# Moving mask adds, query and rotary products to VectorE and key copies to ScalarE in a hybrid two-layer trunk

## The chip, the cores and the metric

The kernel runs on one NeuronCore of a Trainium2 chip. The metric is the device time of one launch in microseconds (us). A core has TensorE (PE in the profile) for matrix products, VectorE (DVE), ScalarE (ACT) and GpSimd (POOL) for elementwise work, and SyncE (SP), which issues the DMA transfers here. Each engine executes its own instructions in the order of the program and waits on semaphores for the others.

## The reference

Two layers run over 640 tokens: 512 of a denoising group and 128 of a context group. Cut to what matters:

```python
h = rmsnorm(x, norm1) * (1 + sc1) + sh1
proj = h @ w_in + b_in          # columns: da_q, da_k, da_v, ml_q..ml_g, na_q, na_k, na_v, merge
# DA: differential attention, 4 heads; rope_2d on q and k of the denoising group; softmax(q1 k1) - lam softmax(q2 k2)
# ML: bidirectional mLSTM, 4 heads, 2 directions; per chunk
sc  = einsum(q, k) * exp(logd - m_t)          # logd is -inf outside the causal triangle
num = inter * einsum(q, c) + einsum(sc, v)    # inter: the decay of the carried state
# NA: neighbourhood attention, 8 heads in 4 pairs, window bias and context keys
x = x + g1 * (merged projections of the three mixers)
x = x + g2 * (relu(h2 @ w_ff1) ** 2 @ w_ff2)
```

All of it is float32; the kernel multiplies in three passes of high and low halves.

## The kernel before, in words

A token tile is 128 tokens; a layer has five, four of the denoising group and one of the context (TT = 5, NT = 640, NS = 512). The weights arrive by DMA in blocks of 1 MB. ScalarE casts a block to its high half (whi, L217), VectorE subtracts to get the low half (wlo, L218), and TensorE multiplies high by high, high by low and low by high (L191 to L193, L210 to L212). The results lie in PSUM banks named mm, of which there are two (NMM = 2); each is evacuated by an instruction of a mixer, such as L620 on VectorE (an mLSTM key plus bias), L454 on ScalarE (a merge gate: bias and tanh), or L501 and L503 on VectorE (merged sums). A new projection group can start when its bank has been evacuated.

A layer runs its mixers as stages: ML, DA, NA, and then the MLP. In each, a driver interleaves the steps of the mixer with projection units for the stage after it, in the order in which the code is traced; a scheduler then orders each engine's instructions by it. In the background of the ML stage VectorE forms the modulation vectors of the next block in chunks of 512 columns (L323, on macc). The four parts of the code that matter:

- **ml_prep** (L732 to L751) fetches what the next head needs: for each of two directions the 128x640 row M (L739, a broadcast DMA from rd), to which a causal mask mlm is added (L741); the 128x512 decay of the queries (L744); and the carried state C. It runs once before the first head, and then within a head (after its second chunk) for the next.
- **ml_stages** (from L753): ScalarE takes exponentials of the masked rows (L768), the scores s = k q are formed, the decays are multiplied with the queries (L776), the scores with the exponentials (L778). Then, chunk by chunk, TensorE updates the state (L808), VectorE adds the decayed old state (L816), TensorE forms the outputs (L826, L828), and VectorE normalises them (L835 to L837, L842, L844). The rotating buffers of the head come from hd().
- **stack** (L919 to L950) prepares keys and queries of a DA head or NA pair. For each half j, the key's high part goes into one half of the partitions of k (L937, and L939 for the 128 cached keys in DA), is copied into the other half (L940); the low part is formed on VectorE (L942, L944) and copied likewise (L945). The copies are 64x640 in DA and 64x512 in NA. Zeroed context keys Kc are formed on GpSimd (L933 to L936).
- **da_rope** (L952 to L959) rotates a head's query or key: a shuffle by 16 partitions (L956), a product with the sines (L957), one with the cosines (L958), and a sum (L959).

In the NA stage GpSimd also forms the window tables (comb, L1216 and L1220), normalises the weights (L1294) and adds gated branches (L504).

Of the kernel before, what the change touches and what calls it, by code (L numbers as in the profile page):

```python
# [11 lines left out]
F32 = mybir.dt.float32  # L12
F32R = mybir.dt.float32r
AF = mybir.ActivationFunctionType
ALU = mybir.AluOpType
# [4 lines left out]
P = 128  # L20
# [3 lines left out]
NS = 512  # L24
NT = 640
TT = 5
# [60 lines left out]
class Builder:  # L87
# [644 lines left out]
    def ml_prep(self, l, h):  # L732
        nc, I = self.nc, self.I
        cv = self.colv[l][0]
        (cA, cB), rd, decb = self.mlc
        Mb, ib, C = [], [], []
        for dr in range(2):
            m = self.hd()
            nc.sync.dma_start(m, rd[0, dr, h].partition_broadcast(P))  # L739
            m3 = m.rearrange("p (c t) -> p c t", c=TT)  # L740
            nc.gpsimd.tensor_tensor(m3, m3, self.mlm[dr].unsqueeze(1).to_broadcast([P, TT, P]), op=ALU.add)  # L741
            Mb.append(m)
            i_ = self.hd()
            nc.sync.dma_start(i_[:, :NS], rd[1, dr, h, 0:NS].partition_broadcast(P))  # L744
            ib.append(i_)
            cst = self.T(self.sp, [P, 129], F32, "C", 8)
            nc.sync.dma_start(cst[:, :P], I["state_ml_C"][0, l, dr, h])
            nc.gpsimd.tensor_copy(cst[:, P:P + 1], cv[:, ROW_SN + 4 * dr + h:ROW_SN + 4 * dr + h + 1])
            C.append(cst)
        return Mb, ib, C  # L750

    def ml_stages(self, l):
        nc, I, O = self.nc, self.I, self.O  # L753
# [8 lines left out]
        for h in range(4):  # L762
            Mb, qs, C = nxt
# [6 lines left out]
            kT, qT = self.mlt.pop(("k", h)), self.mlt.pop(("q", h))  # L770
# [2 lines left out]
                sl = slice(c * P, (c + 1) * P)  # L773
                nc.tensor.matmul(sp[:, sl], kT[:, sl], qT[:, sl], start=True, stop=True)
            for dr in range(2):
                nc.gpsimd.tensor_tensor(qs[dr][:, :NS], qs[dr][:, :NS], qT[:, :NS], op=ALU.mult)  # L776
            for dr in range(2):
                nc.vector.tensor_tensor(Mb[dr], sp[:, :NT], Mb[dr], op=ALU.mult)  # L778
            yield
# [139 lines left out]
    def stack(self, qT, kT, more=None, cache=None):  # L919

        nc = self.nc
        Q, K, Kl = [], [], []
        Kc = self.hd()[:, :512].rearrange("p (j n) -> p j n", j=2)
        nk = NS if more is None else NT
        halves = (slice(0, 64), slice(64, 128))
        for j in range(2):
            a, b = halves[j], halves[1 - j]
            q = self.T(self.sp, [P, NS], F32R, "stq", 2)  # L930
            k = self.T(self.sp, [P, nk], F32R, "stk", 2)
            kl = self.hd(F32R)[:, :nk]
            nc.gpsimd.memset(Kc[b, j], 0.0)  # L933
            nc.gpsimd.tensor_copy(Kc[a, j, :P], kT[a, NS:])
            if cache is not None:
                nc.gpsimd.tensor_copy(Kc[a, j, P:], cache[a])  # L936
            nc.scalar.copy(k[a, :NS], kT[a, :NS])  # L937
            if more is not None:
                nc.scalar.copy(k[a, NS:], more[a])  # L939
            nc.gpsimd.tensor_copy(k[b], k[a].bitcast(F32))  # L940
            nc.scalar.copy(q[a], qT[a, :NS])
            nc.vector.tensor_tensor(kl[a, :NS], kT[a, :NS], k[a, :NS].bitcast(F32), op=ALU.subtract)  # L942
            if more is not None:
                nc.vector.tensor_tensor(kl[a, NS:], more[a], k[a, NS:].bitcast(F32), op=ALU.subtract)  # L944
            nc.gpsimd.tensor_copy(kl[b], kl[a].bitcast(F32))  # L945
            nc.vector.tensor_tensor(q[b], qT[a, :NS], q[a].bitcast(F32), op=ALU.subtract)
            Q.append(q)
            K.append(k)
            Kl.append(kl)
        return dict(qT=qT, Q=Q, K=K, Kl=Kl, Kc=Kc)  # L950

    def da_rope(self, x):  # L952
        nc = self.nc
        cos, sin = self.rope
        sw = self.hd()
        nc.vector.stream_shuffle(sw[:, :NS], x[:, :NS], [i ^ 16 for i in range(32)])  # L956
        nc.gpsimd.tensor_tensor(sw[:, :NS], sw[:, :NS], sin, op=ALU.mult)  # L957
        nc.vector.tensor_tensor(x[:, :NS], x[:, :NS], cos, op=ALU.mult)  # L958
        nc.vector.tensor_tensor(x[:, :NS], x[:, :NS], sw[:, :NS], op=ALU.add)  # L959

# [835 lines left out]
```

## Time and profile before

| | |
|---|---|
| median of 3 runs | 2478.33 us (2477.34 to 2484.72) |
| profiled execution | 2481.89 us, of which the span from the first to the last instruction is 2480.1 us |
| mean granted TensorE clock | 0.994 |
| TensorE busy | 2413.0 us (97%) |
| VectorE busy | 1523.1 us (61%) |
| ScalarE busy | 908.6 us (37%) |
| GpSimd busy | 646.9 us (26%) |

The busy times say how much work an engine had, not whether anyone waited for it. TensorE is busy nearly throughout, so the time is TensorE's work and the places at which it stands still. From the windows one reads how much it stands still in a stretch, from the list of its waits what each of them ended on, and from the timelines what the engine that it waited for was doing. The ML stage of layer 0 lies between 62 and 266 us, its DA stage up to 462 and its NA stage up to 690 us; those of layer 1 follow between 1305 and 1920 us.

### The profile page before, as it was taken

What the parts mean: (1) busy time and instruction counts of PE and PEld (TensorE: products, weight loads), DVE (VectorE), ACT (ScalarE), POOL (GpSimd) and SP (SyncE); (2) the same over time, 40 slices, a digit from 0 to 9 for tenths busy, and PEclk for the clock granted to TensorE, in tenths of its full rate; (3) what the DMA queues carried; (4) which work ended last, traced back from release to release, by engine and by line L of the source; (5) the groups of instructions that cost most, each with busy time, mean ns of one, the idle gap of its engine ahead of it and who ended that gap; (6) DMA issues with size and microseconds to landing.
All of it is one profiled execution on the core that took longest, in us unless ns stands there. A gap on an engine that the chain in (4) does not pass through costs nothing.

```text
span 2480.1 us, 39537 instructions
## 1 busy us (share of the span) xinstructions
PE 2413.0 (97%) x15776; PEld 2265.3 (91%) x15776; DVE 1523.1 (61%) x2788; ACT 908.6 (37%) x1954; POOL 646.9 (26%) x703
## 2 busy tenths in 40 slices
PE   6999999999999999999999999999999999999998
PEld 4999999999998898999989999999989889999997
DVE  5567788566634899998565547664443464444444
ACT  4333344343433422232353334443443353322232
POOL 0122122233412233332022222212351312233301
PEclk8999999999999999999999999999999999999999
DMA  7333323433353334444332322223232722121211
GB/s 268 109 102 110 114 103 131 128 110 129 133 195 126 119 136 151 156 136 153 103 122 98 108 85 80 80 79 114 71 117 85 262 85 85 69 85 69 85 68 60
DMA packets 73706, 286.52 MB, mean 116 GB/s; under 512 B 9889, under 2 KB 21249, under 8 KB 49969
## 3 DMA queue, kind: packets, MB, share of 16 engines
q1 hardware_dynamic: 73520, 283.99, 33.3%
q8 instruction: 124, 2.03, 0.3%
q14 instruction: 62, 0.50, 0.1%
HBM read 257.60 MB, written 26.35 MB: 114 GB/s over the span
## 4 chain that ended last, share of the span: by engine, by line
PE 61%; issue 2%; DVE 2%; POOL 2%; DMA 1%; ACT 1%; SPq 0%; POOLq 0%; DVEq 0%
PE mm L191 9%; PE mm L192 9%; PE mm L193 9%; PE mm L212 4%; PE mm L210 4%; PE mm L211 4%; PE t L210 3%; PE t L212 3%; PE t L211 3%; PE t L193 2%; PE t L192 2%; PE t L191 2%; PE t L1034 1%; PE t L1322 1%; PE s L210 1%
## 5 line engine op out<-in xcount | busy, mean ns | idle before, releaser
L191 PE MATMUL mm<-act,whi 128*128 128x384 f32 (+1 forms) x2160 | 693.0, 321 | 8.2 <-DVE act L503 3.4
L192 PE MATMUL mm<-act,whi 128*128 128x384 f32 (+1 forms) x2160 | 681.4, 315 | 0.0
L193 PE MATMUL mm<-act,wlo 128*128 128x384 f32 (+1 forms) x2160 | 681.1, 315 | 0.0
L217 ACT CAST whi<-raw 128x1024 fp32r<-128x1024 f32 x296 | 310.8, 1050 | 893.7 <-PE mm L192 417.7
L218 DVE TENSOR_TENSOR wlo<-raw,whi 128x1024 fp32r<-128x1024 f32 x296 | 384.0, 1297 | 358.7 <-ACT whi L217 304.9
L191 PEld LDWEIGHTS mm<-act,whi 128*128 128x128 f32 x2160 | 409.7, 190 | 13.2 <-issue 3.8
L192 PEld LDWEIGHTS mm<-act,whi 128*128 128x128 f32 x2160 | 410.0, 190 | 0.0
L193 PEld LDWEIGHTS mm<-act,wlo 128*128 128x128 f32 x2160 | 409.3, 190 | 0.0
L1544 POOL TENSOR_TENSOR x<-x,tmp 128x512 f32<-128x512 f32 x120 | 193.8, 1621 | 449.0 <-DVE tmp L1543 449.0
L210 PE MATMUL mm<-whi,act 128*128 128x512 f32 (+2 forms) x768 | 261.8, 341 | 0.0
L211 PE MATMUL mm<-wlo,act 128*128 128x512 f32 (+2 forms) x768 | 258.2, 336 | 0.0
L212 PE MATMUL mm<-whi,act 128*128 128x512 f32 (+2 forms) x768 | 258.1, 336 | 0.0
L323 DVE SCALAR_TENSOR_TENSOR macc<-raw,cc,macc 128x512 f32<-128x512 f32 x280 | 231.7, 871 | 21.0 <-DMA raw<-w_mod 20.7
L210 PE MATMUL t<-whi,act 128*128 128x512 f32 (+2 forms) x448 | 167.6, 374 | 1.6 <-ACT act L217 1.5
L211 PE MATMUL t<-wlo,act 128*128 128x512 f32 (+2 forms) x448 | 167.0, 373 | 0.0
L212 PE MATMUL t<-whi,act 128*128 128x512 f32 (+2 forms) x448 | 166.8, 372 | 0.0
L212 PEld LDWEIGHTS mm<-whi,act 128*128 128x128 f32 x768 | 146.4, 191 | 14.3
L210 PEld LDWEIGHTS mm<-whi,act 128*128 128x128 f32 x768 | 146.7, 191 | 14.0
L211 PEld LDWEIGHTS mm<-wlo,act 128*128 128x128 f32 x768 | 146.6, 191 | 14.1
L192 PE MATMUL t<-act,whi 128*128 128x256 f32 (+1 forms) x528 | 150.9, 286 | 0.0
L193 PE MATMUL t<-act,wlo 128*128 128x256 f32 (+1 forms) x528 | 150.9, 286 | 0.0
L191 PE MATMUL t<-act,whi 128*128 128x256 f32 (+1 forms) x528 | 150.7, 286 | 0.0
(288 smaller groups left out, 4199.0 us busy)
## 6 DMA issues: line engine op xcount, KB each, us to landing
raw<-w_in SPq DMA_DIRECT2D x64, 1024.0 KB
raw<-w_ff SPq DMA_DIRECT2D x64, 1024.0 KB
raw<-w_mod SPq DMA_DIRECT2D x48, 1024.0 KB
mgd<-act SPq DMA_DIRECT2D x32, 320.0 KB
act<-mgd SPq DMA_DIRECT2D x32, 320.0 KB
raw<-w_out SPq DMA_DIRECT2D x8, 1024.0 KB
gr<-gd SPq DMA_DIRECT2D x12, 512.0 KB
act<-rd SPq DMA_DIRECT2D x16, 320.0 KB
```

Source lines behind the costliest of these rows:

```text
L191: nc.tensor.matmul(o, wh, ah, start=(k == 0), stop=False)
L192: nc.tensor.matmul(o, wh, al, start=False, stop=False)
L193: nc.tensor.matmul(o, wl, ah, start=False, stop=(k == nk - 1))
L210: nc.tensor.matmul(o, ah, wh, start=(first and k == 0), stop=False)
L211: nc.tensor.matmul(o, ah, wlo, start=False, stop=False)
L212: nc.tensor.matmul(o, al, wh, start=False, stop=(last and k == nk - 1))
L217: self.nc.scalar.copy(hi, src)
L218: self.nc.vector.tensor_tensor(lo, src, hi.bitcast(F32), op=ALU.subtract)
L323: nc.vector.scalar_tensor_tensor(acc[v], r3[:, k, :], s, acc[v], op0=ALU.mult, op1=ALU.add)
L1034: nc.tensor.matmul(ops[:, :P], pT[:, j * P:(j + 1) * P], v[:, hsl], start=(j == 0), stop=(j == nb - 1))
L1322: nc.tensor.matmul(ops[64 * j:64 * j + 64], vblk[nmk][:w, h * 64:(h + 1) * 64], zs[j][:w, bi * P:(bi + 1) * P], start=(bi == 0), stop=(bi ...
L1544: nc.gpsimd.tensor_tensor(xs[t][:, sl], xs[t][:, sl], tmp, op=ALU.add)
```

## The change

Five lines go to another engine. The mask add (L741), the product of decays and queries (L776) and the product with the sines (L957) go from GpSimd to VectorE; each is executed 16 times (two layers, four heads, two directions, or query and key). The two copies in stack (L940, L945) go from GpSimd to ScalarE, each 32 times (two layers, DA and NA, four heads or pairs, two halves). Shapes, data and results of each instruction stay as they were.

```diff
 # ml_prep
-            nc.gpsimd.tensor_tensor(m3, m3, self.mlm[dr].unsqueeze(1).to_broadcast([P, TT, P]), op=ALU.add)
+            nc.vector.tensor_tensor(m3, m3, self.mlm[dr].unsqueeze(1).to_broadcast([P, TT, P]), op=ALU.add)
 # ml_stages
-                nc.gpsimd.tensor_tensor(qs[dr][:, :NS], qs[dr][:, :NS], qT[:, :NS], op=ALU.mult)
+                nc.vector.tensor_tensor(qs[dr][:, :NS], qs[dr][:, :NS], qT[:, :NS], op=ALU.mult)
 # stack
-            nc.gpsimd.tensor_copy(k[b], k[a].bitcast(F32))
+            nc.scalar.copy(k[b], k[a].bitcast(F32))
...
-            nc.gpsimd.tensor_copy(kl[b], kl[a].bitcast(F32))
+            nc.scalar.copy(kl[b], kl[a].bitcast(F32))
 # da_rope
-        nc.gpsimd.tensor_tensor(sw[:, :NS], sw[:, :NS], sin, op=ALU.mult)
+        nc.vector.tensor_tensor(sw[:, :NS], sw[:, :NS], sin, op=ALU.mult)
```

The scheduler gives the moved instructions a place in the order of their new engine. The first piece is VectorE's, at the start of layer 0's ML stage. act_815 and act_823 are the masked rows of the two directions, act_866 is a key that L620 evacuates from the projection banks mm_841 and mm_868.

```order
 L728 COPY act_810<-t_804 128x500
 L218 TENSOR_TENSOR wlo_924<-raw_921,whi_923 128x1024
+L741 TENSOR_TENSOR act_815<-act_815,mlm_80_346 128x640
 L620 TENSOR_SCALAR act_866<-mm_841,colv_100 128x256
+L741 TENSOR_TENSOR act_823<-act_823,mlm_81_347 128x640
 L620 TENSOR_SCALAR act_866<-mm_868,colv_100 128x384
 L218 TENSOR_TENSOR wlo_928<-raw_921,whi_927 128x1024
 L218 TENSOR_TENSOR wlo_1060<-raw_1057,whi_1059 128x1024
```

The two mask adds now stand ahead of one evacuation each. In layer 1 the order is the same.

The second piece is VectorE's again, at the fourth head of layer 0's ML stage. act_1906 and act_1914 are its masked rows, act_1909 the decays, macc the background modulation, v_369 a value tile, st_1953 the normaliser.

```order
 L323 SCALAR_TENSOR_TENSOR macc_1839<-raw_2345,cc_89,macc_1839 128x512
 L323 SCALAR_TENSOR_TENSOR macc_1840<-raw_2345,cc_89,macc_1840 128x512
-L323 SCALAR_TENSOR_TENSOR macc_1839<-raw_2345,cc_89,macc_1839 128x512
+L741 TENSOR_TENSOR act_1906<-act_1906,mlm_80_346 128x640
 L885 TENSOR_TENSOR v_369<-mm_1922,vb_366 128x256
-L323 SCALAR_TENSOR_TENSOR macc_1840<-raw_2345,cc_89,macc_1840 128x512
+L776 TENSOR_TENSOR act_1909<-act_1909,act_1571 128x512
+L741 TENSOR_TENSOR act_1914<-act_1914,mlm_81_347 128x640
 L835 TENSOR_TENSOR st_1953<-st_1953,act_810 128x1
 L836 TENSOR_TENSOR st_1953<-st_1953,act_810 128x1
```

The two mask adds and a query product come in between, and two of the background steps (L323) go behind the normaliser's L835.

The third piece is ScalarE's, at the first head of layer 0's DA stage: stk are the doubled keys, stq the queries, act_2723 and act_2736 the keys' low parts, act_2773 a merge gate with its bias.

```order
 L937 CAST stk_2722<-act_2394 64x512
 L937 CAST stk_2735<-act_2394 64x512
+L940 CAST stk_2722<-stk_2722 64x640
 L939 CAST stk_2735<-act_2704 64x128
+L940 CAST stk_2735<-stk_2735 64x640
 L941 CAST stq_2721<-act_2543 64x512
+L945 CAST act_2723<-act_2723 64x640
 L941 CAST stq_2734<-act_2543 64x512
+L945 CAST act_2736<-act_2736 64x640
 L454 ACTIVATE act_2773<-mm_2774,hbias_159 128x256
 L454 ACTIVATE act_2773<-mm_2800,hbias_159 128x384
```

Four copies come in among the casts, all ahead of the two L454.

## Rows read from the trace of the kernel before

**Rows 1.** Busy us by stretch (x instructions), then clock, DMA share, GB/s

```profile
62.00:690.00 628.00, 608.80 (x4448) 591.84 (x4447) 426.38 (x855) 241.18 (x578) 175.52 (x234) 0.99 0.34 116
1305.00:1920.00 615.00, 608.47 (x4465) 593.36 (x4464) 334.17 (x705) 246.69 (x588) 166.39 (x234) 1.00 0.28 93
```

**Rows 2.** TensorE's waits, who for whom: us in total, times, longest us

```profile
PE mm L191 <- DVE act L503: 8.3, 5, 3.4
...
PE t L808 <- DVE act L844: 3.2, 2, 3.0
...
PE t L808 <- DVE C L816: 2.5, 3, 0.8
...
PE mm L191 <- DVE act L501: 1.7, 1, 1.7
PE t L826 <- DVE C L816: 1.6, 2, 1.4
...
PE t L1322 <- DVE act L1309: 1.1, 1, 1.1
...
PE s L1275 <- ACT act L1288: 0.7, 1, 0.7
...
PE mm L191 <- ACT act L454: 0.5, 1, 0.5
```

**Rows 3.** Busy by stretch, as in rows 1, behind the L844 wait

```profile
198.00:201.40 3.40, 3.34 (x16) 3.38 (x17) 2.48 (x8) 0.54 (x2) 1.41 (x3) 0.51 0.61 130
```

**Rows 4.** By line: duration ns min/median/max, first and last start, forms

```profile
L741 POOL TENSOR_TENSOR act<-act,mlm x16: 1537/1580/2526, 87.2 to 1428.1; 128x640 f32<-128x640 f32 x16
...
L776 POOL TENSOR_TENSOR act<-act,act x16: 1260/1294/1852, 96.0 to 1434.5; 128x512 f32<-128x512 f32 x16
...
L957 POOL TENSOR_TENSOR act<-act,rope x16: 1287/1674/1791, 266.8 to 1621.8; 128x512 f32<-128x512 f32 x16
...
L940 POOL CAST stk<-stk x32: 606/720/1266, 271.8 to 1854.4; 64x640 fp32r<-64x640 f32 x16, 64x512 fp32r<-64x512 f32 x16
...
L945 POOL CAST act<-act x32: 607/894/1515, 274.2 to 1859.0; 64x640 fp32r<-64x640 f32 x16, 64x512 fp32r<-64x512 f32 x16
...
L959 DVE TENSOR_TENSOR act<-act,act x16: 674/679/693, 269.2 to 1624.6; 128x512 f32<-128x512 f32 x16
...
L937 ACT CAST stk<-act x32: 602/617/622, 270.0 to 1850.5; 64x512 fp32r<-64x512 f32 x32
```

**Rows 5.** Timelines, layer 0, second head: start us, length us; GpSimd, VectorE

```profile
112.28 1.71 POOL L741 TENSOR_TENSOR act<-act,mlm 128x640 f32<-128x640 f32 x1 [13.25 <-DMA act<-rd]
...
112.75 1.26 DVE L835 TENSOR_TENSOR st<-st,act 128x1 f32<-128x1 f32 x1
113.93 0.15 DVE L836 TENSOR_TENSOR st<-st,act 128x1 f32<-128x1 f32 x1
```

**Rows 6.** Timeline of VectorE, layer 0, fourth head

```profile
189.43 3.39 DVE L323 SCALAR_TENSOR_TENSOR macc<-raw,cc,macc 128x512 f32<-128x512 f32 x3 [0.65 <-DMA raw<-w_mod]
...
193.07 1.45 DVE L323 SCALAR_TENSOR_TENSOR macc<-raw,cc,macc 128x512 f32<-128x512 f32 x1
194.45 1.49 DVE L835 TENSOR_TENSOR st<-st,act 128x1 f32<-128x1 f32 x1
```

**Rows 7.** Timelines at layer 1's first head: GpSimd, VectorE, TensorE

```profile
1325.33 3.11 POOL L741 TENSOR_TENSOR act<-act,mlm 128x640 f32<-128x640 f32 x2 [40.18 <-DMA act<-rd]
...
1320.97 0.48 DVE L620 TENSOR_SCALAR act<-mm,colv 128x256 f32<-128x256 f32 x1 [0.51 <-PE mm L193]
...
1324.93 0.28 PE L191 MATMUL mm<-act,whi 128*128 128x256 f32 x1
```

**Rows 8.** GpSimd's groups (count, busy, mean), 1796 to 1809; VectorE's timeline

```profile
L940 POOL CAST stk<-stk 64x512 fp32r<-64x512 f32 x2 | 1.6, 781 | 6.3 <-ACT stk L937 6.2
L945 POOL CAST act<-act 64x512 fp32r<-64x512 f32 x2 | 1.2, 608 | 0.8 <-DVE act L942 0.8
...
1807.87 0.69 DVE L942 TENSOR_TENSOR act<-act,stk 64x512 fp32r<-64x512 f32 x1 [5.69 <-POOL act L504]
```

## Prediction

> **What bounds the kernel now.** I read the busy times by stretch first, over the two stretches in which the changed lines run: from 62 to 690 us TensorE is busy 608.80 of 628 us, from 1305 to 1920 us 608.47 of 615 us [rows 1]. So the end moves only where TensorE waits. That leaves 19.2 + 6.5 = 25.7 us of idle time, 1.0% of the run; no engine made faster there can gain more. Second, the list of TensorE's waits says how much of it the changed engines own: for VectorE's L503 8.3 us in 5 waits, one of 3.4 us; for L844 3.2 us, one of 3.0; for L816 2.5 and 1.6 us; for L501 1.7 us [rows 2]. They are VectorE instructions of the mixers, and GpSimd stands behind most of them. Third, the clock: behind the L844 wait TensorE runs at a granted 0.51, which is its 1.2 GHz level, for 3.4 us [rows 3], and then at full rate again; the same stands once more, behind the L503 wait, from 1809.1 us on. 3.4 us at half rate are 1.7 us lost, so such a wait costs more than its length.
>
> **What the operations cost.** The 16 mask adds take GpSimd 1580 ns at the median, the 16 query products 1294, the 16 rotary products 1674; the key copies 720 (32 of L940) and 894 (32 of L945) [rows 4]. On VectorE a two-tensor product of the rotary products' size takes 679 ns (L959) [rows 4]; the mask has 640 columns instead of 512, so 0.68 x 640/512 = 0.85 us as an upper bound and 0.68 as the lower; I take 0.85. On ScalarE a 64x512 cast takes 617 ns (L937) [rows 4], so the 64x640 casts of the attention heads lie between 0.62 and 0.77; I take 0.75. So GpSimd gives up about 16 x (1.6 + 1.3 + 1.7) + 64 x 0.8 = 125 us, VectorE takes on 16 x (0.85 + 0.68 + 0.68) = 35 us, ScalarE 32 x 0.62 + 32 x 0.75 = 44 us. VectorE has 1243 - 760.6 = 482 us to spare in these stages and ScalarE 755 [rows 1]. None of these totals is on the path; what counts is where in the queue each instruction stands.
>
> **Mask adds and decayed queries (L741, L776), heads two to four.** Here GpSimd stops VectorE. At 112.28 us it starts a mask add of 1.71 us; VectorE's L835, on 128x1, begins at 112.75 and takes 1.26 us, where L836 of the same shape takes 0.15 right after; it ends at 114.01, as the mask add does at 113.99 [rows 5]. The reciprocal, L816 and TensorE's L808 queue behind it. This is the L808 wait for L816 of at most 0.8 us [rows 2], which stands at the second head of both layers. With the add on VectorE the blocker is 0.85 us of work already in line before, and both waits go: -1.7 us. At the third head of layer 0 the same pair of L816 waits is 0.8 + 1.4 us [rows 2]; its second mask was issued behind the first and lands later, VectorE then waits for it in order, so I credit only half, -1.0. In layer 1 the third head has no such wait now, and VectorE gains one: +0.5 (0 to 1). At the fourth head of layer 0 GpSimd's two adds stretch three L323 to 3.39 us, another to 1.45 and L835 to 1.49 [rows 6], against 0.74 and 0.15, some 1.2 + 0.7 + 1.3 = 3.2 us late; VectorE takes on 0.85 + 0.68 + 0.85 = 2.4 us but drops two L323 behind L835 (second order piece, 1.5 us). Its net lead at L844 is 3.2 + 1.5 - 2.4 = 2.3 us, of TensorE's wait of 3.0 us for L844 [rows 2]; I take 2.2. The rest is too short for what I saw behind the long waits, so the clock dip at 198.0 us goes too: -1.7 [rows 3]. With -0.2 in layer 1 the fourth heads give -4.1.
>
> **The first heads: a new wait.** The masks are fetched just before they are added. In layer 1 GpSimd's adds start when the DMA lands, at 1325.33 us, in layer 0 at 87.2 [rows 4, 7]. In the new order VectorE's add stands ahead of the evacuation L620 that ran at 1320.97 (first order piece). VectorE executes in order, so L620 now comes after 1325.33 + 0.85 = 1326.2 and ends 0.48 later, at 1326.6. Behind it is TensorE: there are two projection banks, and the next group that uses this one began at 1324.93 [rows 7]. It starts 1.7 us late; for layer 0, by the same working, I take 1.3. Sum +3.0. It is the one loss that I can place; if the next bank is late as well it grows to +5.
>
> **Rotary products (L957).** They run beside VectorE's cosine product, and the spread from 1287 to 1791 ns [rows 4] says that the two hold each other up, so I take VectorE's added 0.68 as paid by what it no longer loses there: 0, with 0.7 per head on the path as the bound above. On the path they stand only at the start of layer 0's first head: TensorE waits 1.7 us for L501 there [rows 2], which is queued behind the rotary chain and the key subtractions. I credit -1.2.
>
> **Key copies (L940, L945) on ScalarE.** At a DA start ScalarE gets four casts, 3.0 us, in front of L454, which evacuates the merge gates from the banks (third order piece). At layer 0's first head L454 is waited for already, 0.5 us [rows 2]; the copies push it back by up to 3.0, but the faster rotary products bring the casts forward by about 2, so +1.0, already inside the -1.2 above; in layer 1 +0.3. At the six other DA starts ScalarE has idle time before it, so zero; without that cover 1 us each. In the NA stage the gain is on GpSimd: in layer 1's third head it works in order through L940, window tables, L940, L945 and L504, and VectorE's L942 waits 5.69 us for L504, until 1807.87 [rows 8]; L503 after it is what TensorE's 3.4 us wait is for [rows 2]. The copies that leave this queue ahead of L504 are 1.6 us of L940 and 0.6 of L945 [rows 8], 2.2 us; TensorE's wait shrinks to about 1.2, and the second clock dip goes: -2.2 - 1.7. In layer 0's third NA head the same backlog costs TensorE 0.7 (L1288) and 1.1 us (L1309) [rows 2]: -1.6. NA sum -5.5, to be cut where the extra casts (2.4 us a head) delay the softmax's exponents on ScalarE.
>
> **Sum.** +3.0 (first heads) - 1.7 - 0.5 - 4.1 (second, third, fourth) - 0.9 (DA) - 5.5 (NA) = -9.7 us, against the profiled execution's 2481.89: 2472.2. That execution lies 3.6 us above the median of 2478.33. If the profile adds this always, the median becomes 2478.3 - 9.7 = 2468.6. If instead the two dips (3.4 us) are not in most executions, the median falls by 9.7 - 3.4 = 6.3 to 2472.0. I take the middle, 2470.5.
>
> The Trainium skill speaks against the first group: Perfetto Trace Analysis (Optimizing Scalar/DVE Operations) says that VectorE and GpSimd share a read port, so moving work between the two might not help. By it all L741, L776 and L957 terms but the new wait are zero, and the sum is the rival "given back" below. That L835 is held up until the mask add ends shows the sharing here; whether exchanging 1.6 us on the one for 0.8 us on the other helps, no run shows yet.
>
> **Rivals.** (a) Given back, within 0.3%: the waits for L816 and L844 are not GpSimd's doing but VectorE's own load, so the mask work put in line there returns them: -9.7 + 1.7 + 0.5 + 4.1 = -3.4, or 2475. For it: VectorE is 68% busy in the first of the two stretches [rows 1]. Against it: L835 at 1.26 us and L323 at 1.45 us [rows 5, 6].
> (b) Larger gain: VectorE is stopped by GpSimd at many more places than I walked, and the waits for L503, L844, L816 and L501 go whole: 8.3 + 3.2 + 2.5 + 1.6 + 1.7 = 17.3 us [rows 2], plus 3.4 of clock, less 3.0 at the first heads, -17.7, or 2461 to 2464 by the two readings of the median. For it: GpSimd's own L940 goes from 606 to 1266 ns and L945 from 607 to 1515 [rows 4], so there is contention all over the stages. The Trainium skill, SBUF — State Buffer (SBUF: two separate sides), states the lock in general: the later one of such a pair blocks until the other ends. Against it: most of the waits for L503 have DMA and projection work before them, too.
> (c) Slower: ScalarE's bursts. At 16 head starts 2.4 to 3.0 us of casts go ahead of L454 or the exponents. TensorE waits for L454 already once [rows 2]; if two banks cover only half of the burst everywhere, that is 16 x 1.4 = +22, and the time 2470.5 + 22 = 2492. It ends slower than before from 1 us per start on (16 x 1.0 = 16). Against it: ScalarE works 39% of these stretches, and layer 1's TensorE is idle only 6.5 us [rows 1], so it is covered well so far.
>
> **How the numbers follow.** 0.3% is 7.4 us, about what a measurement of this kernel tells from no change: faster is below 2470.9, slower above 2485.8. Forecast 0.50 (2466 to 2475, of which 0.37 below 2470.9), larger gain 0.11, given back 0.30, slower 0.09. So faster 0.48, same 0.43, slower 0.09. The range takes in all but the tail of the larger gain and the slower case: 2461 to 2480.
>
> **What would show it.** Right: L835 at 0.16 us everywhere, no wait for L816 over 0.3 us at the second heads, none for L844 over 1 us; full clock at 198 and 1809 us; a new TensorE wait of 1 to 2 us at 87 and 1325 us behind VectorE's L620. Wrong: waits for L454 or the exponents at several head starts, first heads' waits above 3 us with a dip of their own, or new dips elsewhere: one such costs as much as any term here.

## The result and the profile after

| | before | after |
|---|---|---|
| median | 2481.15 us (2477.34 to 2484.72, 4 runs) | 2468.18 us (2466.83 to 2469.91, 4 runs) |
| ratio | | 0.9947 (95%: 0.9935 to 0.9959) |
| profiled execution | 2481.89 us, span 2480.1 | 2467.68 us, span 2465.9 |

The change makes the kernel 13.0 us faster, 0.53%. On a second chip, beside its parts (run e7 below), it was 2466.1 against 2480.12 us, ratio 0.9943 (0.9930 to 0.9956). One of the 17 executions of the kernel before on that chip was in a slow state (2944.75 us) and is left out of its median here and below. The forecast was 2470.5 us within 2461 to 2480, with "faster" as the likeliest case.

The busy line of the page after (busy us, share of the span, instructions) says who took the work: ScalarE has 44 us more than before and GpSimd 124 us less, close to the sums of the prediction, but VectorE, which took on 48 instructions, has 5 us less.

```profile
PE 2406.6 (98%) x15776; PEld 2262.9 (92%) x15776; DVE 1517.6 (62%) x2836; ACT 952.4 (39%) x2018; POOL 523.3 (21%) x591
```

So what VectorE no longer lost to GpSimd was more than the 35 us it took on. The list of TensorE's waits after (who for whom, total us, times, longest us) answers [rows 2]:

```profile
PE mm L191 <- DVE act L503: 7.4, 5, 2.4
...
PE mm L191 <- DVE act L620: 3.2, 2, 2.3
...
PE s L1279 <- POOL act L934: 2.0, 3, 0.9
PE mm L191 <- ACT act L454: 1.9, 2, 1.2
...
PE t L808 <- DVE C L816: 1.2, 1, 1.2
...
PE t L808 <- DVE act L844: 0.6, 1, 0.6
PE t L1322 <- DVE act L1309: 0.6, 1, 0.6
```

The waits for L844 fell from 3.2 to 0.6 us, those for L816 from 4.1 to 1.2 in all; the waits for L501 and L1288 are gone. A new one is there, for L620, 3.2 us, and L454 is waited for twice, 1.9 us.

TensorE executes nearly the same order before and after, so the start of the same matrix product in both traces, subtracted, says where time was won. At the ends of the stages (by the time before: 62, 266, 462, 690, 1305, 1500, 1690, 1920 us) the product that began there begins after the change at -0.1, -5.2, -10.4, -12.7, -12.9, -11.1, -10.5 and -14.2 us against before. The differences of these, beside the prediction's terms, and the same for the later runs:

| stage | forecast | after | mask alone (e1) | query alone (e2) | rotary alone (e3) | copies alone (e4) | mask + query (e5) | rotary + copies (e6) | first heads back (e8) |
|---|---|---|---|---|---|---|---|---|---|
| layer 0 ML | -4.4 | -5.1 | -0.9 | -0.5 | -0.3 | +1.3 | -4.0 | -0.6 | -6.3 |
| layer 0 DA | -1.2 | -5.2 | -0.3 | -0.6 | -3.8 | -2.7 | -0.4 | -5.0 | -5.1 |
| layer 0 NA | -1.6 | -2.3 | -1.8 | -1.6 | +1.1 | -1.2 | +4.1 | -0.6 | +0.4 |
| layer 0 MLP | 0 | -0.2 | -0.2 | -0.2 | 0.0 | -0.2 | -0.2 | -0.1 | -0.2 |
| layer 1 ML | +1.1 | +1.8 | +0.7 | +1.0 | -0.1 | -0.2 | +2.2 | -0.4 | -2.0 |
| layer 1 DA | +0.3 | +0.6 | -0.1 | +0.3 | -0.2 | +0.6 | -0.3 | +0.6 | +0.7 |
| layer 1 NA | -3.9 | -3.7 | +0.8 | +0.2 | 0.0 | -2.3 | +0.8 | -2.2 | -2.1 |

Each column is one execution, and executions of one kernel lie up to 10 us apart (before: 2476.4 to 2486.2 us in 32 runs). The clock is part of that: between 62 and 1920 us it falls to the 1.2 GHz level for 3.4 us at 198.1, 478.0 and 1809.2 us in the profile before, at 532.8 and 1314.4 us in this profile of the changed kernel, and only at 466.1 us in its other one (e7). The medians below carry the verdicts, the table says where to look.

**Where GpSimd held VectorE up.** VectorE's timeline after at layer 0's second head answers [rows 5]:

```profile
113.84 0.15 DVE L835 TENSOR_TENSOR st<-st,act 128x1 f32<-128x1 f32 x1
113.91 0.15 DVE L836 TENSOR_TENSOR st<-st,act 128x1 f32<-128x1 f32 x1
```

L835 takes 0.15 us instead of 1.26. At the fourth head [rows 6] had L835 at 1.49 and an L323 at 1.45 us. GpSimd's timeline before says what ran beside them, the query product too and not only the two adds; L835 ended 0.02 us behind the second add. VectorE's L885, which reads a PSUM bank, kept its length beside the query product (last line):

```profile
190.30 1.97 POOL L741 TENSOR_TENSOR act<-act,mlm 128x640 f32<-128x640 f32 x1 [6.49 <-DMA act<-rd]
192.23 1.75 POOL L776 TENSOR_TENSOR act<-act,act 128x512 f32<-128x512 f32 x1
193.93 1.99 POOL L741 TENSOR_TENSOR act<-act,mlm 128x640 f32<-128x640 f32 x1
...
192.74 0.41 DVE L885 TENSOR_TENSOR v<-mm,vb 128x256 f32<-128x256 f32 x1
```

After, the two masks and a query product cost VectorE 0.82 + 0.68 + 0.82 us, and all else keeps its own length:

```profile
189.57 0.82 DVE L741 TENSOR_TENSOR act<-act,mlm 128x640 f32<-128x640 f32 x1
190.30 0.42 DVE L885 TENSOR_TENSOR v<-mm,vb 128x256 f32<-128x256 f32 x1
190.64 0.68 DVE L776 TENSOR_TENSOR act<-act,act 128x512 f32<-128x512 f32 x1
191.24 0.82 DVE L741 TENSOR_TENSOR act<-act,mlm 128x640 f32<-128x640 f32 x1
191.97 0.15 DVE L835 TENSOR_TENSOR st<-st,act 128x1 f32<-128x1 f32 x1
```

**The new wait.** VectorE's and TensorE's timelines after at layer 1's first head, and the window behind (busy us by engine, then the clock), answer [rows 7]:

```profile
1313.26 0.82 DVE L741 TENSOR_TENSOR act<-act,mlm 128x640 f32<-128x640 f32 x1 [5.67 <-DMA act<-rd]
1314.00 0.48 DVE L620 TENSOR_SCALAR act<-mm,colv 128x256 f32<-128x256 f32 x1
...
1314.53 0.58 PE L191 MATMUL mm<-act,whi 128*128 128x256 f32 x1 [2.31 <-DVE act L620]
...
1314.53:1318.00 3.47, 3.47 (x17) 3.47 (x18) 1.35 (x2) 3.47 (x10) 0.00 (x0) 0.53 0.00 2
```

VectorE stands 5.67 us at the mask's DMA with L620 behind it; TensorE waits 2.31 us and then runs 3.5 us at a granted 0.53, its 1.2 GHz level. Together the same products begin 4.0 us later (-12.88 before the place, -8.85 behind it). In layer 0 the wait is 0.9 us, without a dip.

**The DA stage.** Here the forecast was 4 us short. The timelines before at the start of layer 0's second DA head (VectorE, then GpSimd), and TensorE's wait there (300 to 308 us):

```profile
300.81 3.24 DVE L958 TENSOR_TENSOR act<-act,rope 128x512 f32<-128x512 f32 x2
303.97 1.28 DVE L959 TENSOR_TENSOR act<-act,act 128x512 f32<-128x512 f32 x2
305.17 1.54 DVE L1006 TENSOR_REDUCE st<-s 128x1 f32<-128x640 f32 x2
...
300.50 3.00 POOL L957 TENSOR_TENSOR act<-act,rope 128x512 f32<-128x512 f32 x2 [23.04 <-PE s L999]
...
PE s L1021 <- ACT act L1008: 1.6, 1, 1.6
```

Two cosine products that take 0.68 us each alone needed 3.24 us beside GpSimd's two. The softmax's sums L1006 are in line behind them, and for what follows those (L1008) TensorE waited 1.6 us. After, VectorE does all four products itself and reaches L1006 sooner:

```profile
293.00 0.67 DVE L957 TENSOR_TENSOR act<-act,rope 128x512 f32<-128x512 f32 x1
293.60 0.68 DVE L958 TENSOR_TENSOR act<-act,rope 128x512 f32<-128x512 f32 x1
294.20 0.68 DVE L957 TENSOR_TENSOR act<-act,rope 128x512 f32<-128x512 f32 x1
294.80 0.68 DVE L959 TENSOR_TENSOR act<-act,act 128x512 f32<-128x512 f32 x1
295.40 0.68 DVE L958 TENSOR_TENSOR act<-act,rope 128x512 f32<-128x512 f32 x1
296.00 0.81 DVE L1006 TENSOR_REDUCE st<-s 128x1 f32<-128x640 f32 x1
```

From the first product to the start of the first sum it is 4.4 us before and 3.0 us after. Not all of this is the hold-up: after, one of the two L959 stands behind the first sum, which is 0.6 us of it. Up to the end of the second sum, with the same work done, it is 5.9 us before and 5.15 after.

### The profile page after: what moved, and what is told of

Same layout as the page of the kernel before. It is cut to its first block, busy times and chain, and to the rows that moved or that the text cites. A ratio compares the mean times of both kernels' runs of the same rounds, so it can differ in the third digit from the quotient of the medians.

```text
span 2465.9 us, 39400 instructions
## 1 busy us (share of the span) xinstructions
PE 2406.6 (98%) x15776; PEld 2262.9 (92%) x15776; DVE 1517.6 (62%) x2836; ACT 952.4 (39%) x2018; POOL 523.3 (21%) x591
## 3 DMA queue, kind: packets, MB, share of 16 engines
q8 instruction: 124, 2.03, 0.3%
## 4 chain that ended last, share of the span: by engine, by line
PE 80%; DVE 4%; DMA 3%; issue 3%; POOL 2%; ACT 2%; SPq 0%; POOLq 0%; DVEq 0%; ACTq 0%
PE mm L191 13%; PE mm L192 13%; PE mm L193 13%; PE mm L212 4%; PE mm L211 4%; PE mm L210 4%; PE t L210 3%; PE t L211 3%; PE t L212 3%; PE t L192 2%; PE t L193 2%; PE t L191 2%; PE t L1034 1%; PE t L1322 1%; DVE macc L323 1%
## 5 line engine op out<-in xcount | busy, mean ns | idle before, releaser
L323 DVE SCALAR_TENSOR_TENSOR macc<-raw,cc,macc 128x512 f32<-128x512 f32 x280 | 227.5, 856 | 23.3 <-DMA raw<-w_mod 23.1
```

What stands on the lines that cost most here:

```text
L323: nc.vector.scalar_tensor_tensor(acc[v], r3[:, k, :], s, acc[v], op0=ALU.mult, op1=ALU.add)
```

## Experiments

Each run stands beside the kernel before on the same chip; e1 to e4, e5 to e8 and e9 to e12 were on three different chips. Ratios are with their 95% interval.

### The four moves one by one

Each kernel is the one before with one part of the change (e4: both copies).

```diff
 # e1: L741 alone
-            nc.gpsimd.tensor_tensor(m3, m3, self.mlm[dr]...
+            nc.vector.tensor_tensor(m3, m3, self.mlm[dr]...
 # e2: L776 alone
-                nc.gpsimd.tensor_tensor(qs[dr][:, :NS], ...
+                nc.vector.tensor_tensor(qs[dr][:, :NS], ...
 # e3: L957 alone
-        nc.gpsimd.tensor_tensor(sw[:, :NS], sw[:, :NS], sin, op=ALU.mult)
+        nc.vector.tensor_tensor(sw[:, :NS], sw[:, :NS], sin, op=ALU.mult)
 # e4: L940 and L945
-            nc.gpsimd.tensor_copy(k[b], k[a].bitcast(F32))
+            nc.scalar.copy(k[b], k[a].bitcast(F32))
...
-            nc.gpsimd.tensor_copy(kl[b], kl[a].bitcast(F32))
+            nc.scalar.copy(kl[b], kl[a].bitcast(F32))
```

Expected of e1: 

> Only the 16 mask adds (L741) on VectorE. Walked path (my theory: an edit is worth what stood in front of a TensorE wait): a new wait at the two first heads, +1.3 us in layer 0 and +2.3 us and a clock dip of 1.7 in layer 1, against -1.2 and -1.2 at the second heads, -1.3 and -0.5 at the third, -3.8 and -0.5 at the fourth: -3 us in all, 2 to 5. Rival (port: every microsecond taken off GpSimd frees VectorE in proportion): 27 of the 131 us moved, so -3 of -14 as well, but spread over all heads and no gain bound to the fourth head. Rival (given back: VectorE's own load holds TensorE): 0 or slower, +3 to +5, as only the first heads' wait stays.

Expected of e2: 

> Only the 16 query products (L776) on VectorE. Walked path: no TensorE wait stood behind one of them alone except at the fourth and third head of layer 0, where they stretch two VectorE instructions: -0.5 us, between -2 and +1. Port rival: 22 of 131 us moved, -2.4 us. Given back: +0.5 to +2, as VectorE takes on 11 us in its busiest stage.

Expected of e3: 

> Only the 16 rotary products (L957) on VectorE. Walked path: the DA stage of layer 0 gains, as at the first heads' start (-1.2 us) and at the second head, where VectorE's two cosine products took 3.24 us beside GpSimd's (-1.8): -4 us, between -2 and -6, nothing in the ML and NA stages. Port rival: 25 of 131 us moved, -2.7 us. Given back: 0 to +2.

Expected of e4: 

> Only the 64 key copies (L940, L945) on ScalarE. Walked path: -3 us at the third NA head of layer 1 with its clock dip, -1.5 us at that of layer 0, +2.2 us at the second NA head of layer 0, +0.5 to +1 at the DA starts behind L454: -2 us, between 0 and -4. Port rival: 57 of 131 us moved, the largest part, -6 us. ScalarE's bursts as the rival: slower, +2 to +6, with waits for L454 at more than three head starts.

Measured against before's 2480.35 us: e1 2479.76 us, 0.9999 (0.9989 to 1.0009); e2 2480.6, 1.0000 (0.9992 to 1.0009); e3 2478.44, 0.9989 (0.9981 to 0.9998); e4 2475.53, 0.9980 (0.9970 to 0.9991). The differences are -0.6, +0.3, -1.9 and -4.8 us, 7 in all, half of what they give together (taken up behind e8). The mask move is worth nothing alone, short of the 2 to 5 us expected; e2 is within its bounds, e3 just short of its own (2 to 6), e4 beyond (0 to 4), between the walked path and the port rival's -6. That rival fails on e1 and e2, which should have given -3 and -2.4. ScalarE's bursts made e4 no slower.

The trace of e1 at layer 0's second head says why the masks alone gain nothing there. VectorE's and GpSimd's timelines:

```profile
112.99 0.15 DVE L835 TENSOR_TENSOR st<-st,act 128x1 f32<-128x1 f32 x1
113.06 1.25 DVE L836 TENSOR_TENSOR st<-st,act 128x1 f32<-128x1 f32 x1
...
113.00 1.29 POOL L776 TENSOR_TENSOR act<-act,act 128x512 f32<-128x512 f32 x1 [13.78 <-DMA act<-rd]
```

L835 is free, and L836 behind it now takes 1.25 us, to 114.31, 0.02 us behind the end of the query product that is still on GpSimd. The hold-up moved on by one instruction. In e2 it is L835 beside the mask, as before. At the third head it is the moved instruction itself. VectorE's and GpSimd's timelines of e2:

```profile
151.29 2.03 DVE L776 TENSOR_TENSOR act<-act,act 128x512 f32<-128x512 f32 x1 [0.44 <-ACT act L630]
...
151.24 1.53 POOL L741 TENSOR_TENSOR act<-act,mlm 128x640 f32<-128x640 f32 x1 [0.94 <-DVE macc L323]
```

The query product that takes VectorE 0.68 us alone takes 2.03 beside the mask add that stayed, and TensorE waits 2.8 us for L816 behind it. The products behind this head begin 1.8 us later in e2 and 1.0 in e1, each with a clock dip at 155 us, where with both moves (e5) they begin 1.0 us earlier. It is not so everywhere: at layer 0's fourth head the masks alone give 3.2 and the query products alone 2.2 of the pair's 3.7 us, and at layer 1's second head the masks alone give the whole 1.2.

### The two pairs, the whole, and the first heads

e5 has L741 and L776 on VectorE, e6 has L957, L940 and L945 moved, e7 is the changed kernel. e8 is the changed kernel with this edit:

```diff
-            nc.vector.tensor_tensor(m3, m3, self.mlm[dr]...
+            (nc.gpsimd if h == 0 else nc.vector).tensor_tensor(m3, m3, self.mlm[dr]...
```

Expected of e5: 

> Mask adds and query products (L741, L776) both on VectorE, the rest as before. Theory (lock): VectorE is held up as long as any GpSimd instruction of the mLSTM heads is left; alone, the mask move only handed the hold-up of L835 at the second head to L836, behind the query product. So the pair gains more than the two alone (-0.6 and 0 us): -3 to -5 us, with L836 at 0.15 us and the waits for L816 and L844 in layer 0 under 1.3 us each. Rival (additive): -0.3 to -0.6 us, as the two alone give together.

Expected of e6: 

> Rotary products on VectorE and key copies on ScalarE (L957, L940, L945), mask and query work as before. Theory (lock): they share the DA heads' starts, where each alone already removes the same TensorE waits in part, so no more than the sum: -6 to -8 us (alone -1.9 and -4.8). Rival (additive with the other pair's gain located here): -10 us or more.

Expected of e7: 

> The changed kernel once more, beside its parts on one chip. Theory: about -12 us, ratio 0.995, and the two pairs' sum to within 3 us. Additive rival: -7 us, the sum of the four single moves.

Expected of e8: 

> The changed kernel with the mask add of each layer's first head (4 of 16 L741) back on GpSimd; the other 12 on VectorE. Theory: TensorE's waits of 1.1 and 2.3 us for L620 at 87 and 1314 us and the clock dip behind the second go, so 4 to 5 us faster than the changed kernel, -17 us against before. Rival (the first heads' time is bound by the masks' DMA for other reasons, or GpSimd's two adds hold up VectorE's L620 just as long): within 1 us of the changed kernel.

Measured against 2480.12 us: e5 2479.71 us, 0.9999 (0.9991 to 1.0008); e6 2470.82, 0.9961 (0.9948 to 0.9974); e7 2466.1, 0.9943 (0.9930 to 0.9956); e8 2465.56, 0.9937 (0.9924 to 0.9950).

e5 fell against the expectation: -0.4 where 3 to 5 us were expected. Its trace shows the gain and its loss. TensorE's products are 4.0 us ahead at the end of layer 0's ML stage, as the lock theory wants. Then two places give it back. In layer 0's NA stage VectorE's next piece of work is a batch of seven L323, which stands in its queue ahead of evacuations and the window softmax and waits for its weights:

```profile
527.99 5.08 DVE L323 SCALAR_TENSOR_TENSOR macc<-raw,cc,macc 128x512 f32<-128x512 f32 x7 [2.21 <-DMA raw<-w_mod]
```

Before, the same batch began at 529.98 us after 0.67 us of waiting: TensorE comes 3.5 us earlier (at 530 us), the weights only 2.0. TensorE then waits up to 2.5 us for L934 of GpSimd, whose tables wait for VectorE, and a clock dip follows at 542.7; the products fall back 3.4 us there, and the stage ends 4.1 us worse. The second place is layer 1's first head, with 2.3 us and another dip (layer 0's first head, 1.8 us, is already in the 4.0). This profile is one of e5's two slowest executions (2484.23 us), so it shows more loss than the median has. The rival (additive) had the right number for e5. e6's -9.3 us is more than the -6.7 of its parts, against the theory's "no more than the sum", and e7's -14.0 more than the -9.7 of the two pairs, beyond the 3 us expected. But by the spread of the runs e6 cannot be told from the sum of its parts, nor e7 from the sum of the four.

e8 took the waits at the first heads away: its list of TensorE's waits has none for L620 between 60 and 95 or 1295 and 1330 us, and the table shows 1.2 and 3.8 us less in the two ML stages than after (1.0 and 1.5 less than e7's profile, which has no dip at layer 1's first head). But the time went down by 0.5 us only, and the intervals of e7 and e8 lie over each other. In e8's profile layer 0's NA stage is 2.7 us longer than after's and layer 1's 1.6. Both places have a clock dip that after's profile lacks, at 1795.7 us and, for 6.8 us, at layer 0's first NA head (busy us by engine, then the clock):

```profile
464.60:471.40 6.80, 6.19 (x19) 6.19 (x20) 3.61 (x7) 3.93 (x7) 3.94 (x9) 0.50 0.35 108
```

The mean granted clock of every execution says that this is more than one profile's accident: it is 0.9945 on average in e8's six and 0.9955 in e7's, 0.0010 of the span or 2.5 us. An estimate that takes the clock out is the span of each execution times its mean granted clock, averaged; it counts a dip that falls into a wait as if it cost its full half. By it the runs lie from before as follows: e1 -0.7, e2 +0.2, e3 -4.4, e4 -6.7 (sum -11.6); e5 -1.2, e6 -8.7 (sum -10.0); e7 -11.0; e8 -14.7. So e8 is 3.7 us under e7, nearly the 4 to 5 expected, and gave them back to the clock; and the four moves add up to the whole. The half that was missing from their medians is, by this estimate, a matter of the clock (0.9938 and 0.9940 in e3 and e4, 0.9945 in their kernel before), and not of one move needing another, although at single heads one does (e1 and e2 above). Why the clock falls more often in some of these kernels is not shown.

### What the first heads cost, and where the ML gain goes

e9 is e5 with the edit of e8. e10 is the kernel before with finer background steps, e11 is e9 and e12 is e8 with the same:

```diff
-                if kk in ((1, 3, 5) if l else (3,)):
+                if kk in (1, 3, 5):
                     yield
...
-BG_UNITS = range(8, 42, 2)
+BG_UNITS = range(8, 42)
```

Expected of e9: 

> Mask adds and query products on VectorE as in e5, but the mask adds of each layer's first head back on GpSimd; rotary and copies as before. e5 gave 0 although its profile shows 4 us gained in layer 0's mLSTM stage. Theory (given back at three places: the two first heads, 1.7 and 3.9 us with the dip, and the second NA pair of layer 0, 3.4 us with its dip, where seven L323 wait for a weight DMA): without the first heads' waits -3 us, between -1.5 and -5. Rival (mLSTM moves are worth nothing in the median, as the profile of e5 is one disturbed execution): 0, within 1 us of e5.

Expected of e10: 

> The kernel before, with layer 0's background modulation in steps of 4 instead of 8 L323 (twice as many steps, one after every projection unit instead of every second), so that VectorE is not blocked 6 us at a time. Theory: the TensorE wait of 3.0 us for L1182 at 473 us, which stands behind seven L323, shrinks and its dip goes: -2 to -4 us. Rival (the batch follows the DMA, its size doesn't matter): 0, within 1.5 us.

Expected of e11: 

> e9 with the finer background of e10. Theory (the mLSTM gain is given back at the batch of L323 in layer 0's NA stage): it now reaches the end, 5 to 7 us under e10. Rival: as far from e10 as e9 is from before.

Expected of e12: 

> e8 (the changed kernel, first heads' mask adds on GpSimd) with the finer background. Theory: the first two waits of layer 0's NA stage (0.8 to 1.2 and 3.1 us) shrink, 2 to 5 us under e8's 2465.6. Rival: e8's time within 1.5 us, or slower where twice as many background steps get in the way of evacuations.

Measured against 2481.35 us: e9 2474.95 us, 0.9973 (0.9964 to 0.9981); e10 2508.15, 1.0108 (1.0094 to 1.0122); e11 2497.70, 1.0064 (1.0050 to 1.0078); e12 2485.85, 1.0023 (1.0015 to 1.0032).

e9 is 6.4 us faster than before where e5 was level (-0.4), more than the 1.5 to 5 expected: the adds of the two first heads, four instructions of 32 moved, cost the pair what it gains elsewhere. So the pair's zero was no absence of an effect, and without the first heads' adds the ML moves are worth 6 us. In e9's trace the other place is still there: the batch waits 2.12 us for its weights, TensorE 2.4 us for L934, and layer 0's NA stage is 3.3 us longer than before's.

e10 was a failure: 2 to 4 us faster was expected. The wait for L1182 shrank from 3.0 to 2.1 us, but one of 2.8 us for L1180 came beside it and the dip stayed (469.4 us). In layer 0's mixers it is where the kernel before is (-1.6 us at 690 us against -1.3 at 62). It loses 24 us later, in layer 0's MLP, where TensorE now waits for the background sums of layer 1's modulation. Five clock dips come with these waits, between 930 and 1183 us. Its list of TensorE's waits:

```profile
PE t L330 <- DVE macc L323: 10.2, 6, 3.4
```

Why those fall out of step is not shown. For the second NA pair, where e5 and e9 gave back 3.4 and 3.3 us, the traces do answer: with the finer steps the products gain there, 0.5 us in e11 and 1.3 in e12, where they lost 1.4 in e8. In e11 a first NA head that is 3.1 us worse takes that back (TensorE waits 3.4 us for L1182 and 2.5 for L1180); e12 is 14.0 us ahead of before behind layer 0's mixers, e8 11.0. On this base the moves are worth as much or more: e11 is 10.4 us under e10 (5 to 7 expected), e12 22.3 us. But neither is a faster kernel, and e12 is 20 us over e8, where 2 to 5 under it were expected. The fastest measured is e8, level with the changed kernel.

## Why the prediction was right, point by point

**The number had luck in it.** The forecast of 2470.5 stands on a median of 2478.33 us, of three executions; with the fourth it is 2481.15. So the base was 2.8 us too low and the change, -7.8 us forecast and -13.0 measured, 5.2 too small; the two nearly cancel. What held is the mechanism at most of its places, and where it failed is told below.

**Right in size.** The third and fourth heads of layer 0 and the second heads of both: the products behind them begin 1.3, 3.8 and twice 1.2 us earlier, for -1.0, -3.9 and twice -0.85 forecast. The wait for L844 went from 3.0 to 0.6 us with its dip, as forecast. The NA stage of layer 1 gave 3.7 for 3.9, though otherwise than told: VectorE's L942 still waits for L504 of GpSimd, 3.10 us instead of 5.69 [rows 8], and TensorE's wait fell only from 3.4 to 2.4 us, for the 1.2 forecast:

```profile
1795.57 0.79 DVE L942 TENSOR_TENSOR act<-act,stk 64x512 fp32r<-64x512 f32 x1 [3.10 <-POOL act L504]
```

The clock dip behind it went in both profiles of the changed kernel, but it is there in e6's (1802.0 us) and e8's (1795.7 us), with the same wait of about 2.4 us. That 1.7 us is not a property of the order. Layer 0's NA stage has the right number in part by luck too: the third head gave the 1.6 forecast (1.8 measured), but -2.3 for the stage also holds the dip at 478.0 us, which the prediction did not count among the dips before and which this profile lacks (-1.6), and a loss of 2.2 at the second pair.

**Right in place, too small: the first heads.** The term was +1.3 and +1.7; it measured +1.2 (e7: +1.4) in layer 0 and in layer 1 +4.0 with a dip, +1.7 without (e7). Part of that was named as what would prove the forecast wrong, a dip of its own. e9 against e5 prices it at 6.0 us in the median, on the pair alone (2481.35 - 2474.95 less 2480.12 - 2479.71, each against its own kernel before on its own chip).

**Wrong in size: the rotary products.** The step that failed is "I take VectorE's added 0.68 as paid by what it no longer loses there: 0". The row of L957's durations was read as two engines that slow each other down by as much as moving costs. But up to the end of the softmax's second sum it took 5.9 us side by side and 5.15 in line on VectorE, and the second head's wait of 1.6 us for L1008 was not among the rows. The DA stage of layer 0 gave 5.2 us for the 1.2 forecast: 1.8 at the first head, 1.8 at the second, 0.9 at the two others and 0.7 at a wait for L1036. Most of it is the rotary products' own (-3.8 in e3), but the copies, which the prediction gave no gain in DA, have a part: behind the second head's wait TensorE is 1.2 us earlier with the rotary products alone (e3, the wait is 0.4 us), 0.9 with the copies alone (e4), and 1.8 with both (e6, no wait), and the 0.7 at L1036 come with the copies alone (e4).

**Wrong in sign, small: the third head of layer 1** (+0.5 forecast, -0.5 measured) and the second NA pair of layer 0, taken as untouched, which is 2.2 us worse in the trace after, with 1.6 us of waits for L934 instead of 0.9 and a dip at 532.8 (e7: 1.3 us, without a dip there).

**The sum.** On the profiled execution -9.7 was forecast and -14.2 came: 4 us of DA make the difference. On the median the forecast was halved between two readings of the 3.6 us between profile and median. With the median of before at 2481.15, close to the profiled execution, that difference is nearly gone, so there was nothing to halve; -13.0 in the median stands beside -14.2 in the profile.

**The rivals.** "Given back" held in its number for the mask and query moves as long as they stood without the others (e1, e2, e5), but not in its reason: what returned the gain was a batch that waits for its DMA, the first heads, and in e1 and e2 the GpSimd neighbour that stayed. For the whole it fell. (The prediction calls this rival the sum with all L741, L776 and L957 terms at zero; its -3.4 still holds the -0.9 of DA.) "Slower by ScalarE's bursts" fell: TensorE waits for L454 at two places, 1.9 us in all, against 0.5 us before. "Larger gain" came to pass in the DA stage. The Trainium skill, Perfetto Trace Analysis (Optimizing Scalar/DVE Operations), held it possible that moving work between VectorE and GpSimd does not help; e9's 6.4 us says that here it helps; the traces show as its reason that the work on VectorE is shorter than the hold-up it replaces (0.68 us for 1.25 beside a query product). The exclusive lock that the Trainium skill states in SBUF — State Buffer (SBUF: two separate sides) agrees with e1: L836 ended 0.02 us behind the product that held it.

What stays open: why e8, without the first heads' waits, runs at a lower mean clock than e7 and so is not clearly faster. Its one profile shows the loss in the NA stages, at two places where the clock dips come and go from execution to execution.

## What to carry to other kernels

In this kernel an elementwise instruction on GpSimd of 1.3 to 1.7 us was paid a second time by a VectorE instruction beside it with both inputs in SBUF (L835, L836, L323, L958), however small, while L885 with an input in PSUM was not held. Look for 128x1 instructions that take over 1 us, and move the whole group of neighbours: at two of layer 0's heads moving one handed the hold-up to the next, or to the moved instruction itself. Before a moved instruction goes into a fuller queue, look at what it waits for: one that waits for a DMA takes the evacuations behind it along, and leaving just these where they were can be worth as much as the rest of the move. Time won in one stage can be lost in the next where a transfer does not come earlier too. And where a run's clock differs from its neighbour's by 0.001, a difference of 2.5 us between their times need not be the edit's.

## What was not expected of the hardware

The clock did not follow the length of a wait: TensorE's wait of 2.8 to 3.0 us for L1182 before layer 0's first NA head came with a granted 0.5 for 3.4 us in the profile before and in e7 and for 6.8 us in e8, but with none in the changed kernel's first profile (462 us), and a wait of 2.3 us at 1314 us was followed by 0.53 over 3.5 us while one of 2.4 us at 1794 us was not. VectorE got less busy (1523.1 to 1517.6 us) with 48 more instructions in its queue.
